# Sampled attention: cached key pages that arrive with the head's dimension as rows

## The chip, the cores and the metric

The kernel runs on one NeuronCore of a Trainium2 chip. TensorE (PE in the profile) does the matmuls, VectorE (DVE) and ScalarE (ACT) the elementwise work, GpSimd (POOL) some elementwise work and the issue of the indirect transfers, SyncE (SP) the issue of most other transfers. The metric is the time on the device, in microseconds, from the start of the program to its end. What the Python function `kernel()` does with the input arrays before the launch is on the host and is not in that time.

## The reference

One decoding step of a hybrid layer. A prompt of 2048 tokens and eight sampled sequences of eight new tokens each go through a joint input projection; eight "forgetting" attention heads of 64 dimensions and four matrix-memory heads work beside each other; an output projection, a layer norm, a squared-ReLU MLP and a second layer norm follow. The change concerns one part, the attention of the sampled tokens over 8192 cached tokens each:

```python
k_past = cache_k[l][page_table].reshape(DB, past, FOX_HEADS, FOX_HEAD_DIM)
s_past = jnp.einsum('bqhd,bkhd->bhqk', q, k_past).astype(jnp.float32) * scale
s_past = s_past + Ln[..., :, None] + R[:, :, None, :]
```

`cache_k` has 640 pages of 128 tokens x 8 heads x 64 dimensions in float32, 256 KB a page; `page_table` names 64 pages for each of the eight sequences. So 512 pages of keys, 134 MB, are read in the order of the table, and every key is multiplied with the eight queries of its sequence and its head.

## The kernel before

The program is one long list of Python calls that the tile framework turns into instructions. Its stages are: the input projection with the matrix-memory heads beside it (stage A, `block_a`, `m_block`, `m_sample`), the prompt's attention (stage B, `phase_b`), the output projection (stage O, `phase_o`), the MLP (stage C, `phase_c`). The dense matmuls are done as three matmuls of split float32 operands (`mm3`, lines 154 to 156); `split_hi` (line 146, ACT) and `split_lo` (line 149, DVE) make the two halves of each operand.

The sampled attention is a generator, `sample_attention`, that runs in small steps between the pieces of the other stages: each piece of dense work calls `tick` with its rough duration, and whenever these sum up to a pace (5.6 us in stage A, 5 us in stages O and C, none in stage B but for six gathers) the generator does `step(n)`, for n from 0 to 293. In program order a step's instructions stand behind the last dense instruction on each engine. The order on each engine is then fixed when the program is built: `TileContext(nc, schedule_with_timeline_sim=True)` plays the program through with costs of its own, takes the earliest instruction in program order that is ready on an engine, and writes the order down. On the chip each engine works through its list in that order and waits at whatever is not ready.

The steps that matter here, with b for the sequence and g for a group of two key tiles (256 tokens of each of four ranges of the sequence; eight groups a sequence, 64 in all):

- `k_gather(n)` (line 1521): one indirect transfer on POOL's queue. It fetches 128 rows of 4 KB, one into each partition, by the row numbers in column `idxK[:, b, j // 2, j % 2]`, into a slot of a ring (`piece(n)`; four slots in stage A, six from stage B on). There are four a group and 256 in all. A row of `cache_k` is two successive tokens with all their heads and dimensions, so a partition holds tokens.
- `k_turn(n)` (line 1527): two DVE transposes in place, each of a 128x512 half of a piece in blocks of 32x32. Afterwards a partition holds one of 32 dimensions and the blocks lie along the free axis. It is called two steps behind its gather, for two pieces at a time in stage A and for one piece at a time later: 512 transposes in all.
- `qk_step(g)` (line 1550): sixteen matmuls for a group, each with a stationary `qb` of 128x32 and 256 moving columns read out of the ring through an access pattern of 2 x 4 x 32 elements; four of them run beside each other on 32 columns of the array each. They write one PSUM tile, `sQ`, and four fused add-and-maximum instructions on DVE (line 1557) read it.
- `r_load`, `softmax`, `weights`, `v_gather` (line 1638), `pv_step` (line 1662): the forgetting terms, the exponentials, the turned probabilities, the gathers of values and the matmuls with them.

A gather into a slot waits until the matmuls of `qk_step` that read the slot are done. In every stage the turn of a piece stands two steps behind its gather, and the last turn of a group one step ahead of the group's matmuls.

Of the kernel before, what the change touches and what calls it, by code (L numbers as in the profile page):

```python
# [10 lines left out]
F32 = mybir.dt.float32  # L11
# [3 lines left out]
OP = mybir.AluOpType  # L15
# [1368 lines left out]
def sample_attention(tc, I, O, ps_, pps, cst, ident, sqk, dnl, dR, dmix, dqb, vx, kx, pa):  # L1384
# [15 lines left out]
    fo = ps_.tile([128, 8], F32, name="fo")  # L1400
# [2 lines left out]
    V.scalar_tensor_tensor(fo[:, 5:6], fo[:, 1:2], 8.0, fo[:, 2:3], op0=OP.mult, op1=OP.add)  # L1403
    for f in range(2):
        V.tensor_scalar(fo[:, 6 + f:7 + f], fo[:, 0:1], 2.0, float(f), op0=OP.mult, op1=OP.add)
    idxK = ps_.tile([128, 8, 16, 2], I32, name="idxK")
    for a in range(4):
        s = slice(a * 32, a * 32 + 32)
        for f in range(2):
            V.tensor_scalar(idxK[s, :, :, f], ptf[s].rearrange("p (b g k) -> p b g k", b=8, g=4)[:, :, a], 64.0, fo[s, 6 + f:7 + f], op0=OP.mult, op1=OP.add)  # L1410

    idxV = ps_.tile([128, 8, 16, 2], I32, name="idxV")
    for a in range(4):
# [2 lines left out]
            V.tensor_scalar(idxV[s, :, :, f], ptf[s].rearrange("p (b g k) -> p b g k", b=8, g=16)[:, :, :, a], 64.0, fo[s, 6 + f:7 + f], op0=OP.mult, op1=OP.add)  # L1416
    idxL = ps_.tile([128, 4], I32, name="idxL")
    SY.dma_start(idxL, I["page_table"].rearrange("(g b) p -> (b p) g", g=4))
    ck = I["cache_k"][0].rearrange("g (t f) h d -> (g t) (f h d)", f=2)
    cv = I["cache_v"][0].rearrange("g (t f) h d -> (g t) (f h d)", f=2)  # L1420
    cl = I["cache_logf"][0].rearrange("g t h -> g (t h)")
    IO = bass.IndirectOffsetOnAxis
# [67 lines left out]
    GA = 19  # L1490
    NA = 4 * GA

    def piece(n):

        return kx["ring"][:, n // 2 % 2, n % 2] if n < NA else kx["ring"][:, (n - NA) // 2 % 3, n % 2]
# [24 lines left out]
        b, j = divmod(n, 32)  # L1520
        G.indirect_dma_start(out=piece(n), out_offset=None, in_=ck, in_offset=IO(ap=idxK[:, b, j // 2, j % 2:j % 2 + 1], axis=0))  # L1521

    def k_turn(n):

        for i in range(2):
            x = piece(n)[:, i * 512:(i + 1) * 512]
            V.transpose(x, x)  # L1527

    def r_load(g):

        b, kt = divmod(g * 2, 16)
# [4 lines left out]
    def qk_step(g):  # L1536

        b, kt = divmod(g * 2, 16)
        z = state[b]
        rb = z["rb"]  # L1540
        a0 = piece(4 * g)
        d = 1 if g < GA else (2 * (g - GA) + 1) % 3 - 2 * (g - GA) % 3
        pq = pps.tile([128, 2, 256], F32, name="sQ", tag="sX", bufs=1)
        for hg in range(2):
            for db in range(2):
                for h4 in range(4):
                    hd = (hg * 4 + h4) * 2 + db
                    kv = bass.AP(tensor=a0.tensor, offset=a0.offset + hd * 32,
                                 ap=[list(a0.ap[0]), [d * 2048, 2], [512, 4], [1, 32]])
                    r = T.matmul(pq[h4 * 32:h4 * 32 + 32, hg].rearrange("p (k f c) -> p k f c", k=2, f=4), z["qb"][:, hd], kv,  # L1550
                                 start=(db == 0), stop=(db == 1), skip_group_check=True)
        if kt % 4 == 0:
            z["U"].append(ps_.tile([128, 2, 4, 4, 32], F32, name="S", tag="S", bufs=4))
        for k in range(2):
            c = slice(k * 128, k * 128 + 128)
            for hg in range(2):
                V.tensor_tensor_reduce(out=z["U"][kt // 4][:, hg, :, kt % 4 + k], in0=pq[:, hg, c].rearrange("p (b t) -> p b t", t=32),
                                       in1=rb[:, hg, c].rearrange("p (b t) -> p b t", t=32), scale=1.0, scalar=NEG,
                                       op0=OP.add, op1=OP.max, accum_out=z["mx"][:, hg, kt + k:kt + k + 1])
        return r  # L1560
# [133 lines left out]
    def step(n):  # L1694
        after = None
        if n == 0:
            q_load(0)
        g, r = divmod(n - 2, 4)
        if 0 <= g < GA and r >= 2:
            k_turn(4 * g + 2 * r - 4)  # L1700
            k_turn(4 * g + 2 * r - 3)
        if NA + 2 < n < 258:
            if n == NA + 3:
                k_turn(NA)
            k_turn(n - 2)
        g = at(n, 6, 4)
        if g is not None and g < 64:
            after = qk_step(g)
        b = at(n, 35, 32)
        if b is not None and b < 8:  # L1710
            softmax(b)
        p = at(n, 38, 2)
        if p is not None and p < 128:
            pv_step(p // 16, p % 16, after)
        b = at(n, 69, 32)
        if b is not None:
            pv_end(b)
        b = at(n, 37, 32)
        if b is not None and b < 8:
            softmax_new(b)  # L1720
            v_new(b)
        b = at(n, 40, 32)
        if b is not None and b < 8:
            softmax_sum(b)
        for hg in range(2):
            u = at(n, 36 + hg, 8)
            if u is not None and u < 32:
                weights(u // 4, u % 4, hg)
        b = at(n, 30, 32)
        if b is not None and b < 7:  # L1730
            q_load(b + 1)
        b = at(n, 3, 32)
        if b is not None and b < 8:
            q_begin(b)
        g = at(n, 3, 4)
        if g is not None and g < 64:
            r_load(g)
        if n >= 35 and (n % 2 == 1 or not vx["live"]):
            while v_room():
                v_gather()  # L1740
        g, r = divmod(n - 2, 4)
        if 0 <= g < GA and r < 2:
            k_gather(4 * g + 2 * r)
            k_gather(4 * g + 2 * r + 1)
        if NA + 6 <= n < 256:
            k_gather(n)
# [24 lines left out]

# [9 lines left out]
```

## Time and profile before

| | |
|---|---|
| time of the kernel, median of 3 runs | 3441.78 us (3434.79 to 3453.91) |
| span of the profiled execution | 3435.1 us |
| granted PE clock over the span | 0.984 |
| PE busy | 3305.7 us (96%) |
| DVE busy | 2174.9 us (63%) |
| ACT busy | 1365.7 us (40%) |
| POOL busy | 886.5 us (26%) |
| transposes of keys, line 1527 | 512, 330.0 us busy |
| gathers of keys, line 1521 | 256 |

The span is the time from the first to the last instruction of one profiled execution. A time of that execution outside of the span is not given; the fastest of the three runs is within 0.4 us of the span, and the median is 6.7 us above it. Busy times are sums for one engine, so they overlap between engines. In a row that groups instructions the number behind the bar is the busy time, then the mean duration in ns, then the time for which the engine stood idle just before them and what ended it. In a row of the timeline the first number is the start, the second the duration, both in us; the brackets hold the idle time ahead of it and what ended it. PEclk is the share of full clock that TensorE was granted.

### The profile page before, as it was taken

What the parts mean: (1) busy time and instruction counts of PE and PEld (TensorE: products, weight loads), DVE (VectorE), ACT (ScalarE), POOL (GpSimd) and SP (SyncE); (2) the same over time, 40 slices, a digit from 0 to 9 for tenths busy, and PEclk for the clock granted to TensorE, in tenths of its full rate; (3) what the DMA queues carried; (4) which work ended last, traced back from release to release, by engine and by line L of the source; (5) the groups of instructions that cost most, each with busy time, mean ns of one, the idle gap of its engine ahead of it and who ended that gap; (6) DMA issues with size and microseconds to landing.
All of it is one profiled execution on the core that took longest, in us unless ns stands there. A gap on an engine that the chain in (4) does not pass through costs nothing.

```text
span 3435.1 us, 59551 instructions
## 1 busy us (share of the span) xinstructions
PE 3305.7 (96%) x22428; PEld 2682.1 (78%) x22428; DVE 2174.9 (63%) x5286; ACT 1365.7 (40%) x2818; POOL 886.5 (26%) x957
## 2 busy tenths in 40 slices
PE   9999998999989999999999999999999999999998
PEld 8998988888866666677777777777777777888887
DVE  5857757557468887655666667656666545645545
ACT  3333333233358888512323233332333333433332
POOL 0021221322322222276333324323234210100000
PEclk9999999999989999999999999999999999999999
DMA  6565765866653232487877768757669554432221
GB/s 177 141 193 161 238 203 164 271 221 205 224 173 92 74 80 60 154 290 250 292 254 230 260 195 314 267 192 272 230 217 313 197 183 145 164 122 85 82 80 65
DMA packets 428119, 646.37 MB, mean 188 GB/s; under 512 B 84092, under 2 KB 320960, under 8 KB 426936
## 3 DMA queue, kind: packets, MB, share of 16 engines
q1 hardware_dynamic: 351144, 363.35, 35.2%
q0 software_dynamic: 74304, 270.57, 21.5%
q10 hardware_dynamic: 2384, 8.65, 0.7%
q8 instruction: 177, 2.90, 0.3%
q14 instruction: 110, 0.90, 0.1%
HBM read 589.63 MB, written 52.83 MB: 187 GB/s over the span
## 4 chain that ended last, share of the span: by engine, by line
PE 75%; DMA 9%; DVE 6%; issue 5%; ACT 2%; POOL 2%; another core or an unknown queue 0%; SPq 0%; POOLq 0%; ACTq 0%; DVEq 0%
PE py L154 7%; PE py L156 7%; PE py L155 7%; PE ph L156 6%; PE ph L155 6%; PE ph L154 6%; PE po L1022 4%; PE pt L1013 4%; PE pm L154 4%; PE pm L156 4%; PE pm L155 4%; PE sO L1662 3%; PE sQ L1550 3%; DMA kT<-cache_k,idxK 2%; PE pS L974 2%
## 5 line engine op out<-in xcount | busy, mean ns | idle before, releaser
L1345 DVE TENSOR_TENSOR y<-y,py 128x512 f32<-128x512 f32 (+1 forms) x476 | 321.0, 681 | 335.1 <-PE py L156 307.3
L154 PE MATMUL ph<-x1h,wh 128*128 128x512 f32 (+1 forms) x1280 | 455.2, 356 | 3.8 <-ACT wh L146 1.8
L156 PE MATMUL ph<-x1h,wl 128*128 128x512 f32 (+1 forms) x1280 | 452.4, 355 | 3.3 <-DVE wl L149 2.4
L155 PE MATMUL ph<-x1l,wh 128*128 128x512 f32 (+1 forms) x1280 | 453.9, 355 | 1.1 <-DVE x1l L149 0.9
L154 PE MATMUL py<-wh,hh 128*128 128x512 f32 (+1 forms) x1088 | 436.1, 403 | 10.2 <-DVE y L1345 6.9
L1521 POOL DMA_INDIRECT kT<-cache_k,idxK x256 | 263.1, 1028 | 702.2 <-PE sQ L1550 641.6
L146 ACT ACTIVATE wh<-wr 128x1024 fp32r<-128x1024 f32 x268 | 277.5, 1055 | 416.0 <-PE py L156 189.8
L1527 DVE STREAM_TRANSPOSE kT<-kT 128x512 f32<-128x512 f32 x512 | 330.0, 685 | 177.5 <-DMA kT<-cache_k,idxK 161.2
L156 PE MATMUL py<-wh,hl 128*128 128x512 f32 (+1 forms) x1088 | 430.5, 396 | 0.0
L155 PE MATMUL py<-wl,hh 128*128 128x512 f32 (+1 forms) x1088 | 430.5, 396 | 0.0
L149 DVE TENSOR_TENSOR wl<-wr,wh 128x1024 fp32r<-128x1024 f32 x268 | 336.2, 1259 | 70.0 <-ACT wh L146 21.0
L154 PE MATMUL pm<-whi,xh 128*128 128x256 f32 (+2 forms) x1088 | 321.6, 296 | 13.5 <-ACT ch_n L532 4.1
L155 PE MATMUL pm<-wlo,xh 128*128 128x256 f32 (+2 forms) x1088 | 315.6, 290 | 1.2 <-DVE wlo L149 0.8
L156 PE MATMUL pm<-whi,xl 128*128 128x256 f32 (+3 forms) x1088 | 315.0, 290 | 1.2 <-issue 1.2
L154 PEld LDWEIGHTS ph<-x1h,wh 128*128 128x128 f32 x1280 | 241.2, 188 | 45.0 <-issue 6.5
L156 PEld LDWEIGHTS ph<-x1h,wl 128*128 128x128 f32 x1280 | 241.4, 189 | 39.5 <-DVE wl L149 4.6
L155 PEld LDWEIGHTS ph<-x1l,wh 128*128 128x128 f32 x1280 | 241.2, 188 | 37.8 <-issue 2.9
L154 PEld LDWEIGHTS py<-wh,hh 128*128 128x128 f32 (+1 forms) x1088 | 201.2, 185 | 73.0 <-issue 14.1
L156 PEld LDWEIGHTS py<-wh,hl 128*128 128x128 f32 (+1 forms) x1088 | 201.3, 185 | 53.2 <-issue 2.5
L155 PEld LDWEIGHTS py<-wl,hh 128*128 128x128 f32 (+1 forms) x1088 | 201.7, 185 | 44.1 <-issue 2.5
L154 PE MATMUL pm<-xh,whi 128*128 128x256 f32 (+1 forms) x768 | 225.7, 294 | 6.0 <-ACT qi L495 6.0
L1638 POOL DMA_INDIRECT vt<-cache_v,idxV x158 | 165.2, 1046 | 242.7 <-PE sO L1662 162.8
(369 smaller groups left out, 6892.4 us busy)
## 6 DMA issues: line engine op xcount, KB each, us to landing
wr<-w SPq DMA_DIRECT2D x256, 512.0 KB
wra<-w_in SPq DMA_DIRECT2D x112, 512.0 KB
Rb<-dR SPq DMA_DIRECT2D x128, 128.0 KB
xn<-x_prompt SPq DMA_DIRECT2D x16, 512.0 KB
qn<-dq SPq DMA_DIRECT2D x128, 64.0 KB
wr<-w_o SPq DMA_DIRECT2D x16, 512.0 KB
xr<-dmix SPq DMA_DIRECT2D x16, 512.0 KB
y<-x_prompt SPq DMA_DIRECT2D x16, 512.0 KB
```

The lines of the kernel that those rows point to most:

```text
L146: last["ACT"] = A.activation(dst, src, AF.Copy, scale=scale)
L149: r = (eng or V).tensor_tensor(dst, src, hi.bitcast(F32), op=OP.subtract)
L154: T.matmul(ps, wh, xh, start=first, stop=False)
L155: T.matmul(ps, wh, xl, start=False, stop=False)
L156: last["PE"] = T.matmul(ps, wl, xh, start=False, stop=stop)
L1013: T.transpose(pt[:, k], sc[i][0][k0 // 4][:, k * 128:(k + 1) * 128], ident)
L1022: last["PE"] = T.matmul(po[c:c + 64, q0:], z["vn"][:, k], PT[:, k - k0, q0:], start=(k < 2), stop=(k >= nk - 2), skip_group_check=True)
L1345: V.tensor_tensor(y, y, ps, op=OP.add)
L1521: G.indirect_dma_start(out=piece(n), out_offset=None, in_=ck, in_offset=IO(ap=idxK[:, b, j // 2, j % 2:j % 2 + 1], axis=0))
L1527: V.transpose(x, x)
L1550: r = T.matmul(pq[h4 * 32:h4 * 32 + 32, hg].rearrange("p (k f c) -> p k f c", k=2, f=4), z["qb"][:, hd], kv, start=(db == 0), stop=(db == ...
L1638: G.indirect_dma_start(out=vt.rearrange("p f c -> p (f c)"), out_offset=None, in_=cv, in_offset=IO(ap=idxV[:, b, (kt % 4) * 4 + kt // 4, f ...
```

## The change

The keys are laid out another way before the launch, and the transposes on the chip go. `kernel()` turns each page from (token, head, dimension) into (group of four heads, 32 dimensions, head in the group, half of the dimensions, token), that is 64 rows of 4 KB, where the row is named by a group of heads and one of 32 dimensions. The row numbers change with it: piece 0 of a pair of pieces now holds heads 0 to 3 and piece 1 holds heads 4 to 7, where they held even and odd pairs of tokens. `k_turn` and its calls are removed. `qk_step` reads the 256 moving columns as 2 x 128 successive elements in place of 2 x 4 x 32. Number and size of the gathers stay, as do the ring, the steps of all other work and the result.

```diff
+    fk = ps_.tile([128, 2], F32, name="fk")
+    for f in range(2):
+        V.tensor_scalar(fk[:, f:f + 1], fo[:, 0:1], 32.0 * f, None, op0=OP.add)
     idxK = ps_.tile([128, 8, 16, 2], I32, name="idxK")
     for a in range(4):
         s = slice(a * 32, a * 32 + 32)
         for f in range(2):
-            V.tensor_scalar(idxK[s, :, :, f], ptf[s].rearrange("p (b g k) -> p b g k", b=8, g=4)[:, :, a], 64.0, fo[s, 6 + f:7 + f], op0=OP.mult, op1=OP.add)
+            V.tensor_scalar(idxK[s, :, :, f], ptf[s].rearrange("p (b g k) -> p b g k", b=8, g=4)[:, :, a], 64.0, fk[s, f:f + 1], op0=OP.mult, op1=OP.add)
...
-    ck = I["cache_k"][0].rearrange("g (t f) h d -> (g t) (f h d)", f=2)
+    ck = I["cache_k"].rearrange("g f d c -> (g f d) c")
...
-    def k_turn(n):
-
-        for i in range(2):
-            x = piece(n)[:, i * 512:(i + 1) * 512]
-            V.transpose(x, x)
-
...
-                    kv = bass.AP(tensor=a0.tensor, offset=a0.offset + hd * 32,
-                                 ap=[list(a0.ap[0]), [d * 2048, 2], [512, 4], [1, 32]])
-                    r = T.matmul(pq[h4 * 32:h4 * 32 + 32, hg].rearrange("p (k f c) -> p k f c", k=2, f=4), z["qb"][:, hd], kv,
+                    kv = bass.AP(tensor=a0.tensor, offset=a0.offset + hg * 1024 + (h4 * 2 + db) * 128,
+                                 ap=[list(a0.ap[0]), [d * 2048, 2], [1, 128]])
+                    r = T.matmul(pq[h4 * 32:h4 * 32 + 32, hg].rearrange("p (k c) -> p k c", k=2), z["qb"][:, hd], kv,
                                  start=(db == 0), stop=(db == 1), skip_group_check=True)
...
-        g, r = divmod(n - 2, 4)
-        if 0 <= g < GA and r >= 2:
-            k_turn(4 * g + 2 * r - 4)
-            k_turn(4 * g + 2 * r - 3)
-        if NA + 2 < n < 258:
-            if n == NA + 3:
-                k_turn(NA)
-            k_turn(n - 2)
...
+    ck = arrays["cache_k"][0]
+    arrays["cache_k"] = np.ascontiguousarray(
+        ck.reshape(ck.shape[0], 32, 4, 2, 4, 2, 32).transpose(0, 3, 6, 4, 5, 2, 1)).reshape(ck.shape[0], 2, 32, 1024)
```

## The prediction

> **What bounds the kernel now.** I read the page's busy times and its chain that ended last first, then the costliest groups.
>
> ```profile
> PE 3305.7 (96%) x22428; PEld 2682.1 (78%) x22428; DVE 2174.9 (63%) x5286; ACT 1365.7 (40%) x2818; POOL 886.5 (26%) x957
> ...
> PE 75%; DMA 9%; DVE 6%; issue 5%; ACT 2%; POOL 2%; another core or an unknown queue 0%; SPq 0%; POOLq 0%; ACTq 0%; DVEq 0%
> ...
> L1521 POOL DMA_INDIRECT kT<-cache_k,idxK x256 | 263.1, 1028 | 702.2 <-PE sQ L1550 641.6
> ...
> L1527 DVE STREAM_TRANSPOSE kT<-kT 128x512 f32<-128x512 f32 x512 | 330.0, 685 | 177.5 <-DMA kT<-cache_k,idxK 161.2
> ```
>
> TensorE is busy for 96% of the span and makes 75% of the chain; the change takes nothing from it. What goes is the last row: 512 DVE transposes of 685 ns, 330.0 us, and the 161.2 us for which DVE stands at their heads until a gather has landed. DVE has a share of 63%, so most of the 330 us is time that nobody waits for. The question is how much of TensorE's idle time lies behind these transposes. The windows by stage show where they run: from 187 us (the first gather) to 966 us, and from 1423 to 2691 us.
>
> ```profile
> 187.00:966.00 779.00, 727.78 (x6329) 675.37 (x6327) 485.22 (x1299) 264.01 (x577) 205.17 (x233) 0.97 0.66 208
> 966.00:1423.00 457.00, 440.95 (x3011) 304.83 (x3012) 353.62 (x1380) 370.87 (x1028) 126.88 (x205) 0.98 0.32 89
> 1423.00:2691.00 1268.00, 1234.91 (x7658) 924.05 (x7657) 805.62 (x1611) 398.80 (x638) 482.54 (x442) 0.99 0.74 256
> ```
>
> The first number behind the window's length is PE busy. TensorE idles 779 - 727.8 = 51.2 us in the first stretch and 1268 - 1234.9 = 33.1 us in the third. The second, the prompt's attention, has no transposes. So 84 us of idle time is the most that could go, plus what the lowered clock (0.97 and 0.99) costs: 0.03 x 779 and 0.01 x 1268 are 36 us below full clock. That is an outer bound of some 120 us; most of it has other causes.
>
> The view of everything that touches the ring tile names who waits for whom.
>
> ```profile
> L1550 PEldq EVENT_SEMAPHORE  x160: 51/51/2272, 268.9 to 2686.9; - x160
> ...
>   PE sQ L1550: 641.6, 54
> ...
>   DVE kT L1527: 175.9, 79
> ...
>   PE sQ L1550: 3.2, 2
>   PEld mr L350: 1.1, 1
>   PE mr L350: 0.9, 1
> ```
>
> Directly, TensorE waited 3.2 us for the transposes at its own key matmuls, in two places, and 0.9 us at one other matmul. POOL's 641.6 us are gathers that wait for a ring slot, and the slot is freed by TensorE's matmuls, not by DVE. So no gather starts earlier after the change, and nothing that a faster ring could collide with is triggered.
>
> **The change part by part.** *The transposes go.* I looked for each idle stretch of TensorE with transposes ahead of its release on DVE. Four places carry it. The first:
>
> ```profile
> 243.52 0.58 ACT L146 ACTIVATE xh<-px 128x512 fp32r<-128x512 f32 x1
> ...
> 243.49 2.48 DVE L1527 STREAM_TRANSPOSE kT<-kT 128x512 f32<-128x512 f32 x4
> 245.91 0.68 DVE L149 TENSOR_TENSOR xl<-px,xh 128x512 fp32r<-128x512 f32 x1
> ...
> 246.65 0.39 PE L154 MATMUL pm<-whi,xh 128*128 128x256 f32 x1 [3.98 <-DVE xl L149]
> ...
> 243.00:252.00 9.00, 5.36 (x33) 5.36 (x34) 5.98 (x12) 3.25 (x10) 2.92 (x11) 0.81 0.52 173
> ```
>
> Four transposes run between 243.49 and 245.97 us, and only then the split that TensorE waits for. That split needs its ACT half, done at 243.52 + 0.58 = 244.10, so it could start 245.91 - 244.10 = 1.8 us earlier, and the wait of 3.98 falls to 2.2. The clock of that window is 0.81: 9 us x 0.19 / 0.5 = 3.4 us at half clock, which costs 1.7 us. With 2.2 us of wait left it may stay, so I take half of it: 1.8 + 0.85 = 2.7 us (ends 1.8 and 3.5).
>
> ```profile
> 914.95 1.30 DVE L1527 STREAM_TRANSPOSE kT<-kT 128x512 f32<-128x512 f32 x2 [7.36 <-DMA kT<-cache_k,idxK]
> ...
> 918.60 0.65 DVE L677 SCALAR_TENSOR_TENSOR Wm<-mm,Wm 128x512 f32<-128x512 f32 x1
> ...
> 919.30 0.79 PE L687 MATMUL mm<-ident,qk 128*128 128x128 f32 x4 [3.47 <-DVE Wm L677]
> ...
> 916.00:924.00 8.00, 4.70 (x27) 4.70 (x28) 6.79 (x13) 0.86 (x2) 0.00 (x0) 0.79 1.03 383
> ```
>
> Here DVE stands 7.36 us for a gather, and `Wm` is in the queue behind it. With the transposes gone, `Wm` has that time and the whole wait of 3.47 us goes, and with it 8 x 0.21 / 0.5 = 3.4 us at half clock, 1.7 us: 5.2 us.
>
> ```profile
> 762.40 1.31 DVE L1527 STREAM_TRANSPOSE kT<-kT 128x512 f32<-128x512 f32 x2 [2.48 <-DMA kT<-cache_k,idxK]
> ...
> 2518.72 0.94 POOL L1521 DMA_INDIRECT kT<-cache_k,idxK  x1 [0.58 <-issue]
> ...
> 2529.43 1.30 DVE L1527 STREAM_TRANSPOSE kT<-kT 128x512 f32<-128x512 f32 x2 [1.88 <-DMA kT<-cache_k,idxK]
> ...
> 2530.78 0.65 PE L1550 MATMUL sQ<-kT,qb 128*32 128x256 f32 x4 [2.20 <-DVE kT L1527]
> ...
> 2648.24 0.42 PE L1550 MATMUL sQ<-kT,qb 128*32 128x256 f32 x4 [1.05 <-DVE kT L1527]
> ...
> 2523.00:2535.00 12.00, 9.80 (x62) 6.22 (x62) 6.80 (x11) 1.87 (x3) 1.92 (x3) 0.86 0.97 371
> ```
>
> At 762 us the same pair of events holds a matmul for 0.9 us, which goes. At 2530.78 the piece has landed at 2529.43 and is turned from there; the matmul would then wait for the landing itself and start 2530.78 - 2529.43 = 1.35 us earlier. Of the 2.20 us, 0.85 is left, too little for the 12 x 0.14 / 0.5 = 3.4 us at half clock behind it: 1.7 us more. At 2648.24 the wait of 1.05 us is shorter than two transposes of 0.65 and goes. The sum of the places is 2.7 + 5.2 + 0.9 + 1.35 + 1.7 + 1.05 = 12.9 us. The Trainium skill, page "TensorE: Matmul & The Clock Gate", section "HAM oscillation — how this bites in real kernels", warns of idle gaps over about 3.4 us; by that rule alone the gap of 2.20 us could not have lowered the clock and the sum would be 11.2 us, and the trace does not agree, for the lowered clock stands behind it.
>
> *What is late next.* At the key matmuls it is the gather's landing. Between the last gather's issue and the first matmul the trace has 2530.78 - 2518.72 = 12.1 us at the tight place above, and the landing took 2529.43 - 2518.72 = 10.7. The margin grows by 1.3 us where it was tight and nothing else is added: the weight loads of the key matmuls have 160 waits at their sequencer already, of 51 ns in the middle, ahead of the matmuls, since the gathers' own semaphores are waited for on TensorE before the change too.
>
> *The matmuls read otherwise.* 2 x 128 in place of 2 x 4 x 32 moving elements.
>
> ```profile
> L1550 PE MATMUL sQ<-kT,qb 128*32 128x256 f32 x2048 | 129.9, 390 | 3.7 <-DVE kT L1527 3.2 <-issue 0.3
> ...
> L1662 PE MATMUL sO<-vt,PTs 128*32 128x256 f32 x1264 | 86.5, 388 | 5.4 <-DMA vt<-cache_v,idxV 5.4
> ```
>
> The value matmuls have the same shape and read 256 successive elements: 388 ns against 390. I take 0; the ends are 0 and 2 ns x 2048 / 4 (four run beside each other) = 1 us gained.
>
> *The gathers' addresses.* 128 rows of 4 KB as before, but 32 successive rows of a page in place of every other one. Bytes and issues stay. No row shows another spacing, so a landing may become shorter or longer; from the 10.7 us above I allow 10% each way. At the one tight place of stage C that is 1 us, and if there is one such place per sequence, 8 us: I take 0, ends -8 and +8. The two added `tensor_scalar` of one column stand among the index work near 111 us, where such a pair took 0.21 us on DVE:
>
> ```profile
> 111.26 0.21 DVE L1405 TENSOR_SCALAR fo<-fo 128x1 f32<-128x1 f32 x2
> ```
>
> TensorE does not wait there, so 0; without that cover 0.2 us.
>
> *The order.* The planner lays the instructions of each engine anew, with 330 us less on DVE. Which of the other waits this moves cannot be read from the trace. I take 0, with ends of a fifth of the 51.2 us of the first stretch, -10 and +10.
>
> The sum is -12.9 us, plus about 1 us for waits below 1 us: -14. From the profiled span, 3435.1, this is 3421. The median of the runs shown stands 6.7 us above that span, so I put the forecast at 3441.8 - 14 = 3428 us. A measurement of this kernel tells about 0.5% from no change (the three runs lie 19 us apart), 17 us: the forecast is just inside.
>
> **The rivals.** *Hidden anyway.* TensorE's few waits for DVE are taken over by what stands next (ACT for the split at 246 us, the landing at 2530 us) and only the 5.2 us at 919 us show: 3437 us. For it speaks the 96%; against it that two of the places show the transposes as the sole cause. The Trainium skill, page "Perfetto Trace Analysis", section "Identifying Performance Opportunities", says that kernels generally gain by the most contended engine; by that rule this is the outcome, and the rows above show some microseconds beside it.
>
> *More than the transposes.* The freed DVE queue also answers earlier where no transpose stood just ahead. The waits of TensorE for DVE in the two stretches, without those above, are these:
>
> ```profile
> PE py L154 <- DVE y L1345: 6.9, 6, 2.2
> PE px L1150 <- DVE x1l L149: 5.4, 2, 4.5
> ...
> PE px L296 <- DVE xl L149: 6.4, 1, 6.4
> ```
>
> If all went, that would be 18.7 us and, at 1.7 us each, perhaps five stretches of lowered clock, 8.5 us: 3441.8 - 14 - 27 = 3401 us. Against it: no transposes lie in the microseconds ahead of the two longest of them; they would go only by a better order.
>
> *Slower: TensorE takes over DVE's place in the queue.* DVE waited 161.2 us for landings. If the planner, with no transposes to wait for, puts a group's matmuls ahead of where the gathers land on the chip, TensorE stands there, in order, with all dense work behind it. By the mean of the waits behind the transposes' heads (175.9 us in 79, 2.2 us each) and 1.7 us of lowered clock, a stalled group costs 3.9 us. It decides from (14 + 17) / 3.9 = 8 of the 64 groups on; with 15 groups the time is 3441.8 - 14 + 59 = 3487 us. Against it: the matmuls stand three steps of program order behind the last gather, which the change leaves as it is, and before it only two groups were held up.
>
> That the change does not do what it says can hardly be: the calls are gone, and what would be left is a landing that is slower, which is in the third rival.
>
> **How the numbers follow.** Chances: the forecast, 3428 (3418 to 3436), 0.38; hidden, 3437, 0.14; more, 3401 (3387 to 3418), 0.28; slower, 3460 to 3510, 0.20. Faster by over 0.5% means below 3424.6: all of the third case and a quarter of the first, 0.37. Within 0.5%: the rest of the first, the second, and a little of the slower one, 0.45. Slower by over 0.5%: 0.18. The range goes from 3398, which leaves out the better part of the third case (0.08), to 3462, which leaves out most of the slower one: 3398 to 3462. Without the slower case the likeliest has 3408 to 3440, its ends by the terms above.
>
> **What would show it.** Right: no line 1527; DVE busy down by about 330 us to some 1845; TensorE's busy time unchanged within 1%; its idle time in the two stretches down from 84 to about 74 us; the waits of POOL for `sQ` still near 640 us; the waits of DVE for key gathers gone and those of TensorE for them below 5 us. Wrong: TensorE waits for key gathers in many groups (the slower rival), its idle time falls by 30 us or more (the order was worth more than the transposes), or landings much over 10.7 us.

## The result and the profile after

The changed kernel takes 3438.91 us (median of 20 runs, 3429.57 to 3447.60); the kernel before, beside it, 3443.64 (20 runs). The ratio is 0.9987, with an interval of 0.9976 to 0.9997: 4.7 us gained by the medians, where 14 were forecast. On another chip the same program gave 0.9994 (0.9980 to 1.0008). The profiled execution has a span of 3440.4 us, 5 us longer than that of before, so the single spans do not show the gain.

From the page of after, the busy times and the gathers of keys, and from its view of everything that touches the ring tile, who waits for it (us, times):

```profile
PE 3313.8 (96%) x22428; PEld 2676.0 (78%) x22428; DVE 1877.8 (55%) x4776; ACT 1371.0 (40%) x2818; POOL 877.5 (26%) x957
...
L1524 POOL DMA_INDIRECT kT<-cache_k,idxK x256 | 257.1, 1004 | 634.5 <-PE sQ L1547 576.4
...
  POOL kT L1524: 576.7, 56
  DVE S L1554: 54.2, 30
  PE sQ L1547: 6.9, 4
```

Line 1527 is gone and DVE has 297 us less to do. POOL still waits for TensorE, and TensorE waits for key gathers in four places only. PE is busy for 8 us more; nothing that it does has become more.

The windows by stage of before, with the bounds at the same instructions in both kernels: from the first matmul of stage A with gathers beside it to the first of stage B; stages B and O; the three quarters of stage C in which keys are read; the rest. The columns are length, busy PE, PEld, DVE, ACT, POOL (with their instructions), granted PE clock, DMA share, GB/s.

```profile
220.60:966.30 745.70, 694.18 (x6039) 642.27 (x6037) 470.65 (x1247) 253.88 (x554) 195.30 (x220) 0.97 0.66 206
966.30:1657.80 691.50, 664.91 (x4392) 472.14 (x4392) 490.03 (x1688) 426.33 (x1110) 265.30 (x316) 0.98 0.47 151
1657.80:2759.40 1101.60, 1078.91 (x6672) 806.60 (x6671) 704.12 (x1368) 372.53 (x614) 357.57 (x345) 0.99 0.72 249
2759.40:3435.00 675.60, 657.32 (x3677) 554.33 (x3676) 359.90 (x501) 234.23 (x372) 41.24 (x35) 0.99 0.35 113
```

The same of after:

```profile
219.80:949.70 729.90, 689.34 (x6039) 636.47 (x6038) 381.69 (x1090) 254.70 (x549) 198.55 (x223) 0.98 0.67 211
949.70:1643.40 693.70, 666.06 (x4393) 470.76 (x4393) 453.30 (x1623) 427.39 (x1112) 265.75 (x315) 0.98 0.49 150
1643.40:2762.40 1119.00, 1089.01 (x6671) 808.13 (x6672) 531.66 (x1074) 373.98 (x612) 344.90 (x345) 0.99 0.71 244
2762.40:3440.30 677.90, 660.72 (x3677) 555.64 (x3675) 360.13 (x501) 234.59 (x372) 40.91 (x34) 0.99 0.36 113
```

Stage A is 15.8 us shorter, more than the whole forecast. Stage C gives it back: 17.4 us longer while keys are read, with 10.1 us more of PE's busy time for the same matmuls and 7.3 us more of idle time. The other two windows differ by 2 us each. So there are two questions: why does A gain more than the places counted, and what does C lose, where the same transposes went.

### The profile page after: what moved, and what is told of

It reads as the page before. It is cut to its first block, busy times and chain, and to the rows that moved or that the text cites. A ratio compares the mean times of both kernels' runs of the same rounds, so it can differ in the third digit from the quotient of the medians.

```text
span 3440.4 us, 59021 instructions
## 1 busy us (share of the span) xinstructions
PE 3313.8 (96%) x22428; PEld 2676.0 (78%) x22428; DVE 1877.8 (55%) x4776; ACT 1371.0 (40%) x2818; POOL 877.5 (26%) x957
## 4 chain that ended last, share of the span: by engine, by line
PE 47%; DMA 4%; DVE 1%; issue 1%; ACT 1%; POOL 0%; another core or an unknown queue 0%; ACTq 0%; POOLq 0%; DVEq 0%
PE py L154 7%; PE py L155 7%; PE py L156 7%; PE ph L156 7%; PE ph L154 7%; PE ph L155 6%; PE sO L1659 2%; DMA wr<-w 2%; PE sQ L1547 2%; DMA kT<-cache_k,idxK 1%; PE sT L1616 1%; DVE wl L149 0%; DMA y<-dx 0%; PE px L1150 0%; DMA y_prompt<-y 0%
## 5 line engine op out<-in xcount | busy, mean ns | idle before, releaser
L156 PE MATMUL pm<-xh,wlo 128*128 128x256 f32 (+1 forms) x768 | 222.1, 289 | 3.5 <-issue 3.5
```

Of the source, the lines that this page charges most:

```text
L156: last["PE"] = T.matmul(ps, wl, xh, start=False, stop=stop)
```

## Experiments on what the transposes cost

Four kernels, beside each other on one chip, split what a transpose does to DVE's queue (it waits for the landing, and it is busy for 685 ns) and the two stages where it stood.

*The wait alone* (e1_touch_all): the changed kernel, with a copy of one column onto itself where the transposes stood.

```diff
+    def k_turn(n):
+        x = piece(n)[:, 0:1]
+        V.tensor_copy(x, x)
```

> The changed kernel, but DVE copies one column of each gathered piece onto itself where the two transposes stood, so that DVE still waits for every landing (161 us before) and the matmuls still wait for DVE, while the 330 us of transposing stay away. Theory 1, the busy time of the transposes made the 15 us that stage A lost: stage A (up to the first score matmul of the prompt, 966.3 us before and 949.7 after) ends near 950 us and the kernel takes about 3439 us, as the changed one. Theory 2, DVE's wait for landings made them: stage A ends near 963 us, the kernel at about 3444 us. Theory 3, only a new order of the planner moved things: stage A ends anywhere from 945 to 975 us.

*The work alone* (e2_scratch_turns): six transposes of a 128x128 tile in place of the two of a piece; no other instruction of that time needs the tile. It is somewhat more work than before: DVE is busy for 377 us more than in the changed kernel, where the kernel before has 297 more.

```diff
+    def k_turn(n):
+        for i in range(6):
+            V.transpose(tri, tri)
```

> The changed kernel, but DVE does six transposes of a 128x128 tile that nobody reads where the two transposes of a piece stood: about the same busy time, no wait for a landing and no dependency. Theory 1 (busy time): stage A ends near 963 us and the kernel takes about 3444 us or more. Theory 2 (the wait for landings): stage A ends near 950 us, about 3439 us. Theory 3 (order alone): anywhere from 945 to 975 us.

*One stage at a time*: the two transposes of before, called in stages O and C only (e3_turn_c), or in stage A only (e4_turn_a). A piece that is turned holds another order of dimensions than the matmuls read, so these two kernels leave out the right scores of those pieces.

> The changed kernel with the transposes of before put back in stages O and C alone (the scores of those pieces are then of other elements). If stage A gained 15 us by the change and stage C gave 18 to 20 us back because its transposes went, this takes 3444 - 15 = 3429 us, faster than both. If stage C's loss is chance of the order, it takes 3429 to 3445 us. If nothing is tied to a stage, 3439 us as the changed one.

> The changed kernel with the transposes of before put back in stage A alone (the scores of those pieces are then of other elements). If the gain is stage A's and the loss stage C's, this takes 3444 + 18 = about 3458 us, slower than both. If the loss of stage C is chance of the order, 3440 to 3458 us.

Measured against before: the wait alone 1.0022 (1.0007 to 1.0037), the work alone 0.9996 (0.9986 to 1.0006), transposes in C only 1.0059 (1.0041 to 1.0076), in A only 1.0042 (1.0026 to 1.0059). The last came as expected (3458 against 3444 is 1.0041). That the wait alone is slower than the kernel before is a miss: its theories had 3439 or 3444 against 3444. Its profiled execution is within 2 us of the changed kernel's, on another chip, so where the difference lies stays open. The windows of stage A and of stage C with keys, first for e4, with transposes in A only:

```profile
220.80:967.60 746.80, 698.05 (x6039) 643.02 (x6037) 471.81 (x1247) 252.60 (x554) 195.18 (x220) 0.97 0.66 206
1660.60:2773.90 1113.30, 1086.27 (x6671) 807.16 (x6672) 532.46 (x1074) 374.05 (x612) 346.52 (x345) 0.99 0.72 245
```

and for e3, with transposes in C only:

```profile
220.00:940.10 720.10, 684.07 (x6040) 633.19 (x6038) 380.47 (x1086) 254.37 (x549) 199.47 (x220) 0.99 0.68 213
1639.40:2778.10 1138.70, 1103.05 (x6671) 809.79 (x6671) 702.43 (x1368) 373.36 (x613) 344.19 (x345) 0.98 0.70 240
```

Stage A follows the transposes: 746.8 us with them, 720.1 without. With the wait alone it takes 732.4, with the work alone 735.3. It ends at 952.8 and 954.9 us in these two, nearer to the 950 than to the 963 of either theory. In all 20 profiles of this case stage A takes 742 us or more with the transposes of keys and 739 or less without, so neither half alone carries the loss. That a late head and the 1.3 us of work behind it add up is argued, not shown. Stage C does not follow them. It is long in all four, 1109.5 us with the work alone and 1118.1 with the wait alone, and it is longest where the transposes are back: the miss of e3, expected faster than the changed kernel. In e3 TensorE does wait for them, where the kernel before hardly did (3.2 us, two times):

```profile
PE sQ L1553 <- DVE kT L1530: 7.9, 5, 2.4
```

So something in stage C was worse in every kernel made from the changed one, whether it had transposes there or not.

## Experiments on the written order

The planner lays stage C anew in each kernel. To see how much that alone does, PACE_C was moved by 1% in both kernels, which lets the sampled steps in at other places of stage C and changes no work.

```diff
-PACE_C = 5
+PACE_C = 4.95
```

> The kernel before with PACE_C 4.95 in place of 5: the same work, the sampled steps let in among the feed-forward matmuls 1% more often, so that the written order is the same through stage A and B and another in stage C. Theory 'order' (stage C's time hangs on where the planner's order happens to put waits, by more than the 17 us in question): the stretch from the first feed-forward matmul to the last key matmul leaves the 1101.6 us of the kernel before, to somewhere in 1100 to 1140 us, and the time comes out up to 30 us above the kernel before. Rival 'the missing transposes cost in stage C' (with them DVE paces the stage well): with the transposes it stays within 5 us of 1101.6, and the time within 0.2% of the kernel before.

> The kernel before with PACE_C 5.05, 1% less often. Theory 'order': the stretch of stage C with keys again takes another value in 1100 to 1140 us, not the same as with 4.95. Rival 'the missing transposes cost': within 5 us of 1101.6, the time within 0.2%.

> The changed kernel with PACE_C 4.95. Theory 'order': the stretch of stage C with keys leaves 1119 us, somewhere in 1100 to 1140 us, as likely below as above; where it falls to 1102 the time is 3421 to 3427. Rival 'the missing transposes cost': it stays at 1114 to 1124 us and the time at the changed kernel's 3439.

> The changed kernel with PACE_C 5.05. Theory 'order': another value in 1100 to 1140 us. Rival 'the missing transposes cost': 1114 to 1124 us and 3439 us. With the other three runs: by 'order' the two with and the two without transposes overlap in this stretch; by the rival they lie apart by 17 us.

Measured, as ratios to the kernel before: before with 4.95 0.9988 (0.9974 to 1.0001), with 5.05 1.0012 (0.9998 to 1.0025); after with 4.95 0.9979 (0.9969 to 0.9989), with 5.05 1.0001 (0.9989 to 1.0014). An order that nobody chose is worth about 8 us between 4.95 and 5.05, in either kernel, though the intervals of each pair touch or overlap a little. But it does not explain stage C. The windows of stage C with keys for before and for after, both at 4.95:

```profile
1653.00:2738.00 1085.00, 1068.68 (x6688) 802.08 (x6688) 699.28 (x1368) 372.38 (x613) 354.56 (x348) 1.00 0.73 253
```

```profile
1638.30:2739.20 1100.90, 1080.78 (x6687) 802.74 (x6688) 542.51 (x1074) 373.81 (x612) 356.25 (x347) 1.00 0.72 249
```

The pair lies apart by 15.9 us, the pair at 5.05 by 13.4 (1089.6 and 1103.0): nearly the 17.4 of the original pair; of the 15.9, 12.1 are PE's busy time. The lengths of the kernel before, 1085.0 and 1089.6, are ones that neither theory had: they lie below 1100 and over 5 us from 1101.6. This chip is also a faster one, on which the kernel before takes 3424.5 us. The distance within the pairs is what counts, and by it the theory of the order falls as the cause of C's loss. What it was set against, that missing transposes cost in C, had already failed in e3, which has them there and is longest. What was left was the busy time itself.

## Experiments on the addresses

The groups of instructions by line, different shapes apart, show which matmuls became slower. First before, then after, the first matmuls of the MLP (columns: shape, count, busy us, mean ns, idle time before them):

```profile
L154 PE MATMUL ph<-x1h,wh 128*128 128x512 f32 x768 | 304.2, 396 | 2.1 <-ACT wh L146 1.8 <-issue 0.3
L155 PE MATMUL ph<-x1l,wh 128*128 128x512 f32 x768 | 303.2, 395 | 1.1 <-DVE x1l L149 0.9 <-issue 0.2
L156 PE MATMUL ph<-x1h,wl 128*128 128x512 f32 x768 | 301.7, 394 | 2.9 <-DVE wl L149 2.2 <-issue 0.7
```

```profile
L154 PE MATMUL ph<-x1h,wh 128*128 128x512 f32 x768 | 309.6, 403 | 7.2 <-ACT wh L146 5.8 <-ACT x1h L146 1.4
L155 PE MATMUL ph<-x1l,wh 128*128 128x512 f32 x768 | 307.8, 401 | 1.6 <-issue 1.6
L156 PE MATMUL ph<-x1h,wl 128*128 128x512 f32 x768 | 306.7, 400 | 1.9 <-DVE wl L149 1.9
```

Each is 6 to 7 ns slower, 15.0 us over the 2304 of them, in code that the change does not touch. All six kernels made from the changed one so far had 399 to 403 ns here, the three without its new tile 393 to 396. What they share is the tile: `fk`, 8 bytes in each partition, laid out as 32 by the program's addresses, stands in a pool that is filled from the upper end of SBUF, and every tile below it moves down by 32 bytes, the moving operands `x1h` and `x1l` of these matmuls from 77792 to 77760. Their weights `wh` and `wl` lie in a pool filled from the other end and stay. Before, both sides of the matmul began 224 bytes past a multiple of 256; after, the moving side at 192. The second matmuls of the MLP (`py`, 396 to 404 ns in both kernels) have `wh` as the moving side, at 224, and `hh` as the weights, at 96. Four kernels tested this.

*f1_no_tile*: the changed kernel without the tile. The row numbers' second offset goes into a column of `fo` that was written and never read.

```diff
-    V.scalar_tensor_tensor(fo[:, 4:5], fo[:, 0:1], 4.0, fo[:, 1:2], op0=OP.mult, op1=OP.add)
+    V.tensor_scalar(fo[:, 4:5], fo[:, 0:1], 32.0, None, op0=OP.add)
...
-    fk = ps_.tile([128, 2], F32, name="fk")
```

> The changed kernel without its new tile: fk (8 bytes in each partition, laid out as 32) stood above all other tiles of the right-hand side and moved them down by 32 bytes, x1h and x1l of the feed-forward among them (77792 to 77760). Here the two columns of offsets stand in the tile fo that was there before (its column 4 was written and never read), so that every tile has its old address; all else is the changed kernel. In all six kernels with fk that have run the feed-forward's first matmuls (ph, 128x512) take 400 to 403 ns, in the three without it 394 to 396. Theory 'address': they fall to 394 to 396 ns here, 2304 x 6.5 ns = 15 us, the stage of C comes back to that of before, and with stage A's gain of 16 us kept the time is 0.9945 to 0.996 of the kernel before. Rival 'the missing transposes cost in stage C': 401 ns and 0.9987, as the changed kernel.

*f2_before_tile*: the kernel before, with `fk` and its two instructions, read by nothing.

> The kernel before, transposes and all, with the new tile fk and its two instructions added and read by nothing. Theory 'address': the ph matmuls of 128x512 rise from 395 to 401 to 403 ns and the time to 1.004 to 1.005 of the kernel before (15 us). Rival 'the missing transposes cost in stage C': nothing is missing here, 395 ns and 1.000.

*f3_px_pad*: the changed kernel, 32 bytes more in the pool of `x1h` and `x1l` alone.

```diff
+            V.memset(C["px"].tile([128, 8], F32, name="pad", bufs=1), 0.0)
```

> The changed kernel with a tile of 32 bytes more in the pool of x1h and x1l alone: they move another 32 bytes down (77760 to 77728), nothing else moves. Before, x1h and x1l began 32 bytes past a multiple of 64, and 224 past a multiple of 256 like the weights wh and wl they are multiplied by; after, at a multiple of 64. Theory 'address, by 64': at 77728 they are 32 past a multiple of 64 again, ph 395 ns, the time 0.9945 to 0.996 of before. Theory 'address, by 256 against the weights': 160 against 224 is still not the same place, ph stays at 401 ns and the time at 0.9987. Rival 'missing transposes': 401 ns too, so that it falls by the two runs above, not by this one.

*f4_hh_pad*: f1, with 128 bytes ahead of `hh` and `hl`.

```diff
+        V.memset(ph.tile([128, 32], F32, name="pad", bufs=1), 0.0)
```

> The kernel without the new tile (f1) with a tile of 128 bytes ahead of hh and hl, the weights' side of the feed-forward's second matmuls (py): they move from 96 to 224 past a multiple of 256, where the moving wh and wl of these matmuls begin. Theory 'address, by 256 against the weights': py of 128x512 falls from 396 to 403 ns by 5 to 6 ns, 3072 x 5.5 = 17 us, and the time to 0.990 to 0.991 of before. Theory 'address, by 64': py stays, the time is that of f1.

Measured: f1 0.9974 (0.9958 to 0.9990), f2 1.0019 (1.0010 to 1.0028), f3 0.9987 (0.9978 to 0.9997), f4 0.9943 (0.9930 to 0.9957). One row of each, f1, f2 and f3 for `ph`, f4 for `py`:

```profile
L155 PE MATMUL ph<-x1l,wh 128*128 128x512 f32 x768 | 303.4, 395 | 0.2 <-issue 0.2
```

```profile
L155 PE MATMUL ph<-x1l,wh 128*128 128x512 f32 x768 | 306.2, 399 | 1.8 <-issue 1.8
```

```profile
L155 PE MATMUL ph<-x1l,wh 128*128 128x512 f32 x768 | 307.2, 400 | 1.5 <-issue 1.5
```

```profile
L155 PE MATMUL py<-wl,hh 128*128 128x512 f32 x1024 | 403.0, 394 | 1.5 <-DVE wl L149 1.5
```

The durations move as the theory says in all four, in f2 by less than expected (398 to 400 ns, where 401 to 403 were). And f2, which has all its transposes, takes 1115.0 us in stage C where the kernel before takes 1101.6: nothing is missing there but the old addresses. f3 puts the moving side at 160 past a multiple of 256 and 32 past a multiple of 64, and stays slow, so that 64 is not the unit. f4 makes matmuls fast that had never been so (`py` 395 to 405 ns in every kernel above). The times follow with less than expected: f1 came back by 4 to 5 us against the changed kernel beside other runs, not by 10 to 15, and f2 lost 6.5 where 15 were expected. The written order hardly differs in these pairs: against the changed kernel f1 has one matmul in another place and a few instructions of VectorE, f3 only its memsets; against the kernel before f2 has one matmul and one instruction of VectorE in another place. But f1's ten executions lie 29 us apart, so the time itself was measured again.

First the changed kernel and f1 once more, beside each other, and the same 128 bytes put into the kernel before (g2_before_hh):

> The changed kernel as it is, once more, beside the next run on the same chip. Expected: 0.9987 of before again; the ph matmuls of 128x512 at 400 to 403 ns. If the idle time of TensorE in stage C while keys are read is again near 31 us (before: 23), the written order makes it; if it falls by 5 us or more, it was that execution.

> The changed kernel without the 8-byte tile, once more. Theory 'address': it is faster than the run beside it by the 9 to 15 us of the ph matmuls, 0.996 to 0.997 of it, so 0.9945 to 0.996 of before. Rival: address costs hardly anything of the time (other waits take it over): within 0.1% of the run beside it.

> The kernel before with the 128-byte tile ahead of hh and hl, so that the weights' side of the py matmuls begins 224 past a multiple of 256, as its moving side does. Theory 'address': py of 128x512 falls by 3 to 6 ns, 3072 x 4.5 = 14 us, 0.996 of before, with all transposes in place. Rival (only together with the change): 1.000.

The changed kernel gave 3441.19 us (0.9994, 0.9980 to 1.0008), the one without the tile 3430.44 (0.9969, 0.9955 to 0.9983), the kernel before with the 128 bytes 0.9973 (0.9961 to 0.9985). By the medians the tile costs 10.8 us here, by the ratios 8.6. In the first measurement f1 and f3, beside each other, are 4.5 us apart by the ratios and 1.6 by the medians, and f2 lost 6.5. So the tile costs some 4 to 9 us; its size is not known better than that. The cure of `py` is worth 9 us without the change, where 14 were expected, and here the written order is that of the kernel before with one memset more. The idle time of stage C in the second profile of the changed kernel is 1113.5 - 1086.5 = 27.0 us, 3 below the first, which decides for neither case of the expectation, from this row:

```profile
1643.70:2757.20 1113.50, 1086.49 (x6670) 806.74 (x6671) 532.06 (x1074) 373.69 (x612) 342.75 (x345) 0.99 0.72 245
```

Then two kernels with the same written order on all engines, f4 with 256 and with 384 bytes in place of 128. They differ in the size of one memset and in the addresses of `hh` and `hl` (and of `mhs` and `mls`, which share their place):

> The changed kernel without the 8-byte tile, with 256 bytes ahead of hh and hl in place of 128: their start is 96 past a multiple of 256 as it was without any, while wh and wl begin 224 past. The written order is that of the kernel with 128 bytes. Theory 'address, by 256 against the weights': py of 128x512 is back at 397 to 405 ns, the time 13 us above the next run, 0.997 of before. Rival 'any move of hh helps, or another modulus': py stays at 393 to 401 ns and the time at 0.994.

> The same with 384 bytes: 224 past a multiple of 256 again, like wh and wl. Theory 'address, by 256 against the weights': py of 128x512 at 393 to 401 ns as with 128 bytes, 0.994 of before, and 13 us below the run beside it. Rival 'another modulus (512 or more)': 397 to 405 ns and 0.997.

```profile
L154 PE MATMUL py<-wh,hh 128*128 128x512 f32 x1024 | 412.8, 404 | 9.1 <-DVE y L1344 7.7 <-issue 1.4
L155 PE MATMUL py<-wl,hh 128*128 128x512 f32 x1024 | 406.0, 396 | 0.0
L156 PE MATMUL py<-wh,hl 128*128 128x512 f32 x1024 | 405.7, 396 | 0.0
```

```profile
L154 PE MATMUL py<-wh,hh 128*128 128x512 f32 x1024 | 409.3, 401 | 9.0 <-DVE y L1344 7.3 <-issue 1.4 <-DVE y L1346 0.2
L155 PE MATMUL py<-wl,hh 128*128 128x512 f32 x1024 | 402.9, 393 | 1.0 <-DVE wl L149 1.0
L156 PE MATMUL py<-wh,hl 128*128 128x512 f32 x1024 | 402.0, 393 | 0.0
```

With 256 bytes (weights at 96, moving side at 224) 3434.25 us, 0.9983 (0.9969 to 0.9998); with 384 (both at 224) 3419.19 us, 0.9943 (0.9927 to 0.9959). That is 15 us from addresses alone, in one order, on one chip (the medians; by the ratios 14), and 10.3 us of it stand in the busy time of the three rows.

The mean of such a row counts each matmul up to a modelled end, and successive matmuls overlap. The starts are recorded as such. From the start of one matmul of 128x512 to the start of the next of the same output, the median in each of the 20 profiles (lines 154 to 156 together) is this:

| group | same place modulo 256 | another place |
|---|---|---|
| `ph` | 227 ns, in 10 profiles | 233 to 234 ns, in 10 |
| `py` | 227 ns, in 4 (f4, g1, g2, 384 bytes) | 232 ns, in 16 |
| `pw` | 227 ns, in 1 (g1) | 232 ns, in 19 |

No profile falls out of line. For the 3072 matmuls of `py` 5 ns make 15 us, the difference of the last two kernels; by the means of all distances under 400 ns, 236.7 and 233.0, it is 11 us. One gap is left for `ph`: f1 moved its moving side back together with all other tiles that lie below `fk`, and f3 moved it alone, but to another slow place. That it is this operand is argued from `py` and `pw`.

*What gained, together* (g1_best): the changed kernel without the tile, 128 bytes ahead of `hh` and `hl` and of stage O's `mh` and `ml`, and PACE_C 4.95.

> What gained, together: the changed kernel without the 8-byte tile, 128 bytes ahead of hh and hl, the same ahead of mh and ml (the weights' side of stage O's 768 pw matmuls, 5 ns each: 4 us), and PACE_C 4.95 (4 us on the chip where it ran). Expected by adding up from the 0.9943 of the kernel with the first two: 8 us less, 0.992 of before (3416 where before takes 3443). If the order of stage C takes the part of PACE_C back: 0.994.

It takes 3417.46 us, 0.9922 (0.9909 to 0.9935), 27 us less than the kernel before and the fastest found. By the ratios that is 7 us below f4, where 8 were expected. The part for stage O does not show in its rows: the `pw` matmuls have 396 to 408 ns, with 306.9 us in all against 308.5 before, where 4 us were expected. It shows in the starts, 227 ns apart in place of 232, which is 4 us over 768 matmuls.

Stage lengths of the profiled executions and the mean of the three `ph` rows, for some of the kernels above, one execution each (us and ns; "tile" says whether `fk` is there):

| kernel | transposes in | tile | stage A | stage C, keys | ph, ns | ratio |
|---|---|---|---|---|---|---|
| before | A, C | no | 745.7 | 1101.6 | 395 | 1 |
| f2 | A, C | yes | 748.7 | 1115.0 | 399 | 1.0019 |
| e4 | A | yes | 746.8 | 1113.3 | 401 | 1.0042 |
| e3 | C | yes | 720.1 | 1138.7 | 402 | 1.0059 |
| after | none | yes | 729.9 | 1119.0 | 401 | 0.9987 |
| after, again | none | yes | 729.2 | 1113.5 | 400 | 0.9994 |
| f1 | none | no | 738.7 | 1107.6 | 395 | 0.9974 |
| f1, again | none | no | 731.0 | 1105.9 | 395 | 0.9969 |
| h, 256 bytes | none | no | 732.2 | 1103.5 | 397 | 0.9983 |

## Why the prediction was wrong

The time lies in the stated range and within 0.5% of the kernel before, as forecast, but the size was wrong: 14 us, of which 4.7 were measured. Three terms were off, and not the same way: stage A gained more than was counted, stage C gained nothing, and the new tile, taken at 0, cost 4 to 9 us. That the time came out no further from the forecast is luck.

*The step that failed: "the two added `tensor_scalar` of one column ... so 0".* The lines that make the second offset were costed by their instructions, which cost nothing. The tile that they write was not costed at all, and it moved the operands of 2304 matmuls off the place of their weights modulo 256. Between kernels that differ by it, beside each other, that is 4.5 us (f3 and f1), 6.5 (f2 and before) and 8.6 (the changed kernel and f1 again) by the ratios. Without the tile the change gives 0.9974, 0.9969 and, with 256 bytes of harmless padding, 0.9983: a mean of 0.9975, 8.6 us of 3443, of the 14 forecast. My line "TensorE's busy time unchanged within 1%" could not catch this: 3313.8 against 3305.7 is 0.25%, and it is more than the gain that was measured.

*The places in stage A: right in the two that carry it.* Two rows of after, at the split of the first place and at the matmul that had waited for `Wm`, and the windows around them:

```profile
243.06 0.39 PE L154 MATMUL pm<-whi,xh 128*128 128x256 f32 x1 [2.32 <-DVE xl L149]
...
900.70 0.60 PE L687 MATMUL mm<-ident,qk 128*128 128x128 f32 x4
...
240.60:249.60 9.00, 6.68 (x57) 6.54 (x56) 5.55 (x11) 4.68 (x13) 2.81 (x11) 1.00 0.57 194
896.00:904.00 8.00, 8.00 (x70) 8.00 (x70) 1.12 (x4) 1.23 (x3) 3.50 (x5) 1.00 0.97 340
```

The first wait fell from 3.98 to 2.32 us (2.2 forecast) and the lowered clock went whole, not by half: 1.7 + 1.7 = 3.4 us, the upper end. The second went with its lowered clock: 5.2 us as forecast.

*"Four places carry it": too few.* Without transposes stage A is 13.5 to 25.6 us shorter in the kernels of the table (7.0 in f1's first profile), where I had counted 8.8. I had searched for TensorE's waits for DVE. The list of what TensorE waited for before has waits for ACT in stage A as well (us in total, times, longest):

```profile
PE pm L154 <- ACT qi L495: 6.0, 2, 5.7
...
PE pm L154 <- ACT ch_n L532: 4.1, 1, 4.1
```

All six kernels with transposes of keys in stage A have such waits, and none of the thirteen without has them there at 2 us or more. Followed back, the second stands behind transposes, over two engines (rows of the timeline of before):

```profile
809.53 2.49 DVE L1527 STREAM_TRANSPOSE kT<-kT 128x512 f32<-128x512 f32 x4
811.93 0.71 DVE L504 SCALAR_TENSOR_TENSOR ac<-qi,cw,ac 128x512 f32<-128x512 f32 x1
813.09 3.52 DVE L504 SCALAR_TENSOR_TENSOR ac<-qi,cw,ac 128x512 f32<-128x512 f32 x5
815.25 0.63 ACT L505 ACTIVATE qi<-ac 128x512 f32<-128x512 f32 x1 [8.96 <-DVE ac L504]
820.10 0.56 ACT L532 COPY ch_n<-px 3x512 f32<-3x512 f32 x1
820.71 0.58 PE L154 MATMUL pm<-whi,xh 128*128 128x256 f32 x1 [4.14 <-ACT ch_n L532]
```

Four transposes (2.5 us) stand in the middle of the convolution on DVE, ACT stands 8.96 us for its end, and the copy that frees TensorE's PSUM tile comes late in ACT's queue. How much of the 4.14 us is the transposes' share is not shown by these rows. The other wait, at 556 us, has a transfer of weights ahead of it, and its chain was not followed. But the kernel with the work alone has it, and the one with the wait alone has not, so it hangs on the transposes' work (e2, stage A):

```profile
PE pm L154 <- ACT qi L495: 4.6, 1, 4.6
```

The clock is at half for 6.8 us around the first of these waits and for 3.4 us behind the second. The two waits with the work done at that clock are some 14 us, an estimate from these rows. With the 8.6 us of the two places above that is more than the 15.8 by which stage A is shorter, so other waits took a part of it back.

*The places in stage C: not a gain.* The forecast for the 58th of the 64 groups, at 2530 us, was that 0.85 of its 2.20 us would be left and the lowered clock would go. In after the same group stands longer, for the landing itself:

```profile
2498.93 0.94 POOL L1524 DMA_INDIRECT kT<-cache_k,idxK  x1 [0.57 <-issue]
...
2511.86 1.41 PE L1547 MATMUL sQ<-kT,qb 128*32 128x256 f32 x16 [3.54 <-DMA kT<-cache_k,idxK]
```

From the second of the four issues to the matmul these are 12.9 us, where they were 12.1, and 3.4 us at half clock follow, as before. So "what is late next" had the right cause, and the 1.35 + 1.7 us did not come. In the second execution of the changed kernel this wait is 0.61 us, so its size changes from run to run. The 1.05 us at 2648 became 0.65. In stage C of after TensorE waits in all for landings, and for a row of `y`:

```profile
PE py L154 <- DVE y L1343: 7.1, 1, 7.1
PE sQ L1547 <- DMA kT<-cache_k,idxK: 6.2, 3, 3.5
PE ph L154 <- ACT wh L146: 4.3, 1, 4.3
```

At equal addresses stage C is 1103.5 to 1107.6 us without transposes against 1101.6 with them, and with `py` cured 1100.8 (f4 and 384 bytes) against 1097.5 (g2): 2 to 6 us lost where 4 were forecast as gained. Two executions of the changed kernel differ by 5.5 us there (1119.0 and 1113.5), so that no gain came is all that is shown. Why stage C is perhaps a little worse stays open.

*"The matmuls read otherwise", taken as 0*, was right: 389 ns against 390 over the 2048 key matmuls.

*"The order", taken as 0 with 10 each way*, was about right in size: PACE_C moved by 2% is worth 8 us, in stage C alone.

*The rivals.* None of them is what happened. "Hidden anyway" had the time, 3437, but not the mechanism: what the transposes cost was not hidden, it was gained in stage A and spent on addresses. "Slower, TensorE takes over DVE's place" did not come: 6.9 us in four places. "More" was right on the side of stage A only.

*The signs.* DVE is busy for 297 us less, not 330: neighbours on DVE overlap by some 0.06 us (the transposes at 243.49 end at 245.97, the next row starts at 245.91), which is about 31 us over 512, an estimate. TensorE's idle time, in the windows of stage A and of stage C with keys, fell from 74 to 71 us, where a fall of 10 was forecast for its stretches. POOL's waits for `sQ` are 576 us and not near 640, and TensorE's for key gathers 6.9 us and not below 5; neither was followed.

The Trainium skill, page "SBUF — State Buffer", section "Specifications (TRN2)", gives SBUF cachelines of 16 bytes, with a penalty for each cross to a new line. By that alone a move of 32 bytes, two whole lines, would change nothing, and the rows of `ph` do not agree: 396 ns became 403. The page's section "Operand start alignment" asks for a start at a multiple of the element's size and says of itself that it is about legality and not about speed; all starts here are such.

## What to carry to other kernels

A new tile, however small, moved every tile that was laid out after it on its side of the memory: look at the mean duration of the big matmuls, shape by shape, and better at the time from start to start, before reading any difference as the change's own. Where two versions must be compared to 0.3%, keep the addresses, or time both with and without a pad. And when work goes from a queue, follow TensorE's waits back over a second engine: the wait named last need not be for the engine that was late.

## What was not expected of the hardware

Matmuls of 128x512 float32 with 128 columns of weights follow each other some 5 to 7 ns sooner when their moving side and their weights begin at the same place modulo 256 bytes of their partitions: 227 ns from start to start, against 232 to 234. This holds in all three groups (`ph`, `py`, `pw`) of all 20 profiles. For the rows of line 155, which follow another matmul of their own accumulation, the mean durations say the same: `ph` took 393 to 396 ns in the kernels with the same place and 399 to 402 in those without, `py` 393 to 394 and 396 to 398. Moving sides at 192 and 160 against weights at 224, and 224 against 96, were all slow. Moving sides of 288 columns show nothing clear: 295 ns in before and in after, though in before only every other one of them, those on columns 0 to 287, had the same place as its weights. Whether it is the two sides' distance or the place 224 itself that counts is not told apart: all fast pairs of 512 had both at 224. Why it is so stays open.

The lowered clock does not go by the length of the gap ahead of it alone: 2.20 us at 2530 us in before was followed by 3.4 us at half clock, 2.32 us at 243 us in after by none.
